# Splitting 32 weight blocks and the memory during the gates' stage, and a new order in the mixer's first group

## The chip, the cores and the metric

The kernel runs on one core of a Trainium2 chip. The time is device time in microseconds (us) of one execution, and a run's result is the median of its executions. A core has TensorE (PE, matmul; PEld is its weight load), VectorE (DVE), ScalarE (ACT), GpSimd (POOL) and SyncE (SP, which here only issues DMA loads). Each takes its instructions in order.

## The reference

Two blocks, 1024 tokens by 1024 features, all in fp32. The change touches the first block's gates and output, and the second block's mixer and cross-attention memory:

```python
m = sigmoid(g_att) * y_att + sigmoid(g_conv) * y_conv      # gates
x = x + m @ w_out                                          # first block's end, then a norm
proj = rmsnorm(x) @ w_in_2                                 # mixer: q_a k_a v_a q_i k_i w_i q_b k_b v_b
out_a = dsa_attention(...)   # index scores, top 256 keys of a query, softmax over those
out_b = diff_attention(...)  # (softmax(q1 k1) - lam softmax(q2 k2)) v, 4 heads
h = x + concat(out_a, out_b) @ w_out_2
k, v = rmsnorm(mem) @ w_xk, rmsnorm(mem) @ w_xv            # mem: 256 rows, for cross-attention
```

## The kernel before

A matmul of fp32 precision is made of three in fp32r: each operand is **split** into a high part (`hi`, an ACT copy that rounds, L130) and a low part (`lo = x - hi`, a DVE subtraction, L133, or L136 with a scale), and `mm3` (matmuls at L189) sums hi·hi, lo·hi and hi·lo. Activations and weights are both split, in tiles of 128 x 1024. `w` (L178) loads a weight block from DRAM into the one buffer `wr`, and splits it into `wh` and `wl` (two buffers each).

SBUF tiles come from tags with a fixed number of buffers: `U` 32, `P` 6, `PT` 4, `wr` 1, `wh` and `wl` 2, and in PSUM `S` 2, `T` 2, `A` 1, `D` 1. A new tile of a tag waits until an old one was read for the last time. `load` (L158) is a DMA issued by SP; it can be held back by `ago(ns)` until a matmul that lies that far back on PE. `dspill` (L174) stores a tile in DRAM by a DMA that POOL issues.

The stages in order of time, in us of the profiled execution:

- 358 to 675, **gates**: 16 iterations `end(n)` of seven products of four k-steps (a fast matrix product with sums of operands), 12 x 7 matmuls of 512 columns, 19.3 us each. PE's order is the written one. Sums and gate functions lie on DVE and ACT and use six `P` tiles; results go to DRAM.
- 675 to 807, the convolution's product, and **wo1**: `for d in range(8)` in `block1` multiplies by one block of w_out, adds x (`P`), splits the result into `hn2[d]` (`U`), sums its squares in `acc1` and `acc2` and spills it.
- 807 to 1086, **mixer projections**. A group (`tok_group`) has two weight blocks (`kh` 0 and 1, on hn2[0..3] and hn2[4..7]) and eight token tiles, 192 matmuls. The groups are w2b (196 columns: k_i, k_a, v_a, w_i), w2i (q_i), two each of w2q, w2k, w2v and w2a. `ahead` prepares weights two groups ahead, through `wr`, alternately into `U` and into `wh`, `wl`. In the w2b group `rms1` and `rms2` (column sums of acc1 and acc2 on PE, then DVE and POOL) give the factor `r12` with which all results are scaled. After w2i come the index scores (888 to 912), then 31 steps of the search for the top 256: one step counts on ACT (`jka`, three tiles) and DVE (`jkd`, three tiles) and updates the threshold `C`, on which the next step depends. The steps are woven between the groups' results, which `rope` copies from PSUM with ACT and turns on DVE. Before the last group `diff_prep` transposes q and k of the first head (L1126), for which a `T` buffer is needed.
- 1086 to 1500, **attention**: `diff`, 4 heads x 8 query tiles, with the last part of the search (`topk_final`), then `dsa`. Into it `weave` mixes at rate 0.43 `mem_in` (loads and splits the memory, sums its squares), `mem_kv` (16 weight blocks wkv, each loaded and split by `w`) and `ob_part`.
- then output products, cross-attention and the conv-GLU, which the change doesn't touch.

Except where the order is written (gates), a scheduler lays out each engine's and SP's order from the program's order and its own model of times.

Of the kernel before, what the change touches and what calls it, by code (L numbers as in the profile page):

```python
# [98 lines left out]
class Kernel:  # L99
# [216 lines left out]

    def mem_in(self, d, cost):

        m = []
        for q in range(2):  # L320
            x = self.big("U")
            self.load(x.rearrange("p (k c) -> p k c", k=4), self.I["memT"][4 * q:4 * q + 4].rearrange("k p c -> p k c"),
                      self.ago(4000))
            m += [x[:, c * 256:c * 256 + 256] for c in range(4)]
        for q in range(2):
            h, l = self.big("U", F32R), self.big("U", F32R)
# [84 lines left out]
    def tok_group(self, wv, x, ncols, small=False, inner=False, ws=None, mid=None):  # L411
# [390 lines left out]
    def mixer(self):  # L802
# [682 lines left out]
    def gates(self, attg):  # L1485
# [359 lines left out]
```

## Time and profile before

| | |
|---|---|
| median of 3 runs (lowest, highest) | 2467.7 us (2466.17, 2472.75) |
| the profiled execution's own time | 2467.37 us |
| its span | 2465.6 us |
| mean granted TensorE clock | 0.978 |
| busy: PE, DVE, ACT, POOL | 95%, 66%, 50%, 9% |

The span runs from the first to the last instruction; 1.8 us of the time lie around it. A granted clock of 1.00 is 2.4 GHz, 0.50 is 1.2 GHz. The shares are means over stages that differ much, so a stage is read from its own window.

### The profile page before, as it was taken

How to read it: one execution, taken by the hardware profiler on the slowest of the kernel's cores; microseconds unless marked ns; L12 is line 12 of the kernel's file. 1: busy time of each engine (PE TensorE's matmuls, PEld its weight loads, DVE VectorE, ACT ScalarE, POOL GpSimd, SP SyncE). 2: the span in 40 equal slices, each digit the busy share in tenths (PEclk: the TensorE clock that was granted, in tenths of full speed). 3: DMA queues.
4: the chain of work that ended last, by engine and by line, in shares of the span. 5: the costliest groups of instructions: out<-in, count | busy, mean ns of one | idle time of the engine just before them, and what ended most of it. 6: DMA issues, size and time to landing. Idle time of an engine off the chain costs nothing.

```text
span 2465.6 us, 32347 instructions
## 1 busy us (share of the span) xinstructions
PE 2340.9 (95%) x12324; PEld 1982.7 (80%) x12324; DVE 1631.2 (66%) x2666; ACT 1231.2 (50%) x2070; POOL 211.1 (9%) x318
## 2 busy tenths in 40 slices
PE   8999989999999899957798999999999999999999
PEld 7887878888888899956687777887878888888887
DVE  5476785565565478789976886435578888875433
ACT  4465554333433367788676764335454445543231
POOL 0000020000000114131111110000000000000000
PEclk9999999999999899989899999999999999999999
DMA  4323363312444222243452225212322222225554
GB/s 141 101 67 114 94 216 148 110 65 72 171 143 145 84 67 76 84 133 107 137 165 77 88 78 191 81 49 79 135 77 87 84 77 77 86 86 188 172 179 145
DMA packets 91548, 275.91 MB, mean 112 GB/s; under 512 B 11392, under 2 KB 16896, under 8 KB 91392
## 3 DMA queue, kind: packets, MB, share of 16 engines
q1 hardware_dynamic: 75168, 216.45, 27.2%
q0 software_dynamic: 15792, 57.15, 6.2%
q8 instruction: 97, 1.59, 0.3%
q14 instruction: 59, 0.48, 0.1%
q10 hardware_dynamic: 432, 0.23, 0.1%
HBM read 187.81 MB, written 64.49 MB: 102 GB/s over the span
## 4 chain that ended last, share of the span: by engine, by line
PE 74%; DVE 11%; ACT 6%; issue 4%; DMA 2%; POOL 2%; SPq 0%; DVEq 0%; ACTq 0%; POOLq 0%
PE S L189 39%; PE T L189 12%; PE D L189 11%; PE A L189 9%; DVE U L133 2%; PE T L493 2%; ACT jka L130 2%; DVE P L133 1%; ACT P L130 1%; DMA U<-sp 1%; DVE PT L133 1%; DVE jkd L1067 1%; DVE P L486 1%; ACT U L130 1%; POOL st L221 1%
## 5 line engine op out<-in xcount | busy, mean ns | idle before, releaser
L189 PE MATMUL S<-U,wh 128*128 128x512 f32 x1792 | 582.7, 392 | 18.5 <-ACT U L130 8.4
L189 PEld LDWEIGHTS S<-U,wh 128*128 128x128 f32 x1792 | 338.5, 189 | 92.7 <-ACT U L130 8.4
L189 PE MATMUL S<-U,wl 128*128 128x512 f32 x896 | 351.3, 392 | 2.9 <-DVE wl L133 2.9
L189 PE MATMUL D<-U,wh 128*128 128x512 f32 x816 | 281.3, 398 | 0.2
L130 ACT ACTIVATE wh<-wr 128x1024 fp32r<-128x1024 f32 (+1 forms) x113 | 112.7, 998 | 312.7 <-PE D L189 169.9
L133 DVE TENSOR_TENSOR wl<-wr,wh 128x1024 fp32r<-128x1024 f32 (+1 forms) x113 | 130.9, 1159 | 170.2 <-ACT wh L130 170.1
L189 PE MATMUL S<-U,U 128*128 128x256 f32 (+6 forms) x1040 | 216.0, 335 | 13.5 <-DVE st L486 12.7
L189 PE MATMUL S<-U,PT 128*128 128x512 f32 x912 | 224.8, 395 | 0.7 <-ACT jkd L130 0.7
L189 PEld LDWEIGHTS S<-U,PT 128*128 128x128 f32 x912 | 171.1, 188 | 41.9 <-ACT jkd L130 1.4
L189 PEld LDWEIGHTS S<-U,wl 128*128 128x128 f32 x896 | 169.4, 189 | 40.6 <-DVE wl L133 4.7
L189 PEld LDWEIGHTS S<-U,U 128*128 128x128 f32 x1040 | 159.5, 199 | 30.8 <-DVE st L486 14.5
L189 PEld LDWEIGHTS D<-U,wh 128*128 128x128 f32 x816 | 152.0, 188 | 29.6 <-DVE U L133 1.5
L189 PE MATMUL D<-U,wl 128*128 128x512 f32 x408 | 160.8, 394 | 0.4 <-DVE wl L133 0.4
L189 PE MATMUL T<-U,wh 128*128 128x512 f32 x480 | 161.0, 390 | 0.0
L189 PE MATMUL S<-wh,U 128*128 128x256 f32 x768 | 142.2, 287 | 0.0
L130 ACT ACTIVATE P<-P,st 128x640 f32<-128x640 f32 (+7 forms) x168 | 124.1, 739 | 35.8 <-DVE st L486 34.3
L130 ACT ACTIVATE PT<-T 128x512 fp32r<-128x512 f32 (+4 forms) x208 | 110.2, 544 | 53.7 <-PE T L493 46.5
L130 ACT ACTIVATE wh<-U 128x1024 fp32r<-128x1024 f32 x73 | 77.4, 1060 | 114.1 <-PE T L189 51.9
L133 DVE TENSOR_TENSOR wl<-U,wh 128x1024 fp32r<-128x1024 f32 x73 | 89.2, 1222 | 65.4 <-ACT wh L130 65.4
L133 DVE TENSOR_TENSOR PT<-U,PT 128x1024 fp32r<-128x1024 f32 x74 | 67.7, 955 | 97.7 <-PE S L189 97.7
L189 PE MATMUL A<-U,wh 128*128 128x512 f32 x368 | 125.1, 390 | 0.0
L189 PEld LDWEIGHTS S<-wh,U 128*128 128x128 f32 x768 | 122.2, 195 | 0.0
(298 smaller groups left out, 4660.7 us busy)
## 6 DMA issues: line engine op xcount, KB each, us to landing
U<-sp SPq DMA_DIRECT2D x73, 512.0 KB, 4.3
P<-sp SPq DMA_DIRECT2D x56, 512.0 KB, 4.5
sp<-P POOLq DMA_DIRECT2D x56, 512.0 KB, 2.9
sp<-U POOLq DMA_DIRECT2D x51, 512.0 KB, 3.5
U<-in_wf SPq DMA_DIRECT2D x43, 512.0 KB, 3.5
U<-in_w SPq DMA_DIRECT2D x30, 512.0 KB, 3.2
U<-U SPq DMA_DIRECT2D x116, 128.0 KB, 2.4
wr<-in_wf SPq DMA_DIRECT2D x23, 512.0 KB, 3.6
```

The costliest lines, as they stand in the source:

```text
L130: return self.nc.scalar.activation(out, in_, f, **kw)
L133: return self.nc.vector.tensor_tensor(out, a, b, op=op)
L189: self.last = self.nc.tensor.matmul(out, l, r, start=start, stop=stop, skip_group_check=True)
L221: self.nc.gpsimd.tensor_tensor(y, v, self.mhalf[:, :n], op=OP.pow)
L486: self.nc.vector.tensor_tensor_reduce(pv, v, add.rearrange("p (n x) -> p n x", n=n), scale, BIG, OP.add, OP.min, nm)
L493: self.nc.tensor.transpose(T[:, j * 128:j * 128 + 128], b, self.ident)
L1067: self.nc.vector.tensor_scalar(self.junk["d"][:, :w], SD[i], C[:, j:j + 1].bitcast(F32), None, op0=OP.is_lt, op1=OP.add, accum_out=cnt[:, ...
```

## The change

Of the weights, 16 blocks of the mixer (w2q, w2k, w2v, w2a) and the 16 blocks of wkv are now split early by `presplit`: loaded, split, and both parts stored in DRAM. 23 of them go into the gates' iterations (through `P`, one or two in an iteration, none in the last two), 9 into wo1 (through `U`). Later `parts` loads the two parts where the block was loaded and split before. The memory is split, squared and summed in gates n = 5 and 9 (`mem_split`). The low part is written over the loaded block. The weights of w2b are loaded and split in wo1 (d = 7). In the w2b group the second weight block's matmuls run k = 0..2 for all token tiles first, and k = 3, which reads hn2[7], last; rms1 comes after the first token tile of that pass, and rms2 after the fourth.

```diff
+    def presplit(self, key, tag):
+        ap = self.I[key[0]][key[1:]]
+        x, hi = self.load(self.big(tag), ap, self.ago(6000)), self.big(tag, F32R)
+        lo = x.bitcast(F32R)
+        self.split(hi, lo, x)
+        self.halves[key] = [self.dspill(v.bitcast(F32)) for v in (hi, lo)]
+
+    def parts(self, key, tags=("wh", "wl"), gate=None):
+        r = [self.t(t, [128, 1024], F32R) for t in tags]
+        for x, d in zip(r, self.halves[key]):
+            self.load(x.bitcast(F32), d, gate)
+        return r
...
+    def mem_split(self, q):
+        x, hi, sq = self.big("P"), self.big("P", F32R), self.big("P")
...
+        self.act(sq, x, AF.Square)
+        self.tt(sq[:, :512], sq[:, :512], sq[:, 512:], OP.add)
...
+        for c in range(4):
+            sl = slice(c * 256, c * 256 + 256)
+            self.split(hi[:, sl], lo[:, sl], x[:, sl], scale=self.gv("mem", 4 * q + c))
+        self.halves["mem", q] = [self.dspill(v.bitcast(F32)) for v in (hi, lo)]
...
-        for k in range(8):
-            self.split(*d[k], m[k], scale=self.gv("mem", k))
-            self.add_sq(acc, m[k], k == 0)
-            yield cost
+        acc = self.msq
+        yield cost
...
-                wh, wl = self.w(self.I["wkv"][which, h, kh])
+                wh, wl = self.parts(("wkv", which, h, kh))
...
+            if key + (kh,) in self.halves:
+                ws[kh] = self.parts(key + (kh,), (tag, tag) if tag else ("wh", "wl"))
+                continue
...
+        if mid is not None:
+            order[8:] = [(1, tt, range(3)) for tt in range(8)] + [(1, tt, range(3, 4)) for tt in range(8)]
...
+            if d == 7:
+                self.first = self.tok_weights(("w2b",), "U")
...
+            for _ in range((2, 2, 2, 2, 1, 0, 0, 0)[d]):
+                self.presplit(self.early.pop(0), "U")
...
+            for _ in range((1, 1, 2, 2, 2, 1, 2, 2, 2, 1, 2, 2, 2, 1, 0, 0)[n]):
+                self.presplit(early.pop(0), "P")
+            if n in (5, 9):
+                self.mem_split(n // 9)
```

**PE at the start of the w2b group.** `A` is the column sums, `S_6604` or `S_6932` the last product of wo1, `S_6716` or `S_7044` w2b's first PSUM tile. Before:

```order
L189 MATMUL S_6604<-U_6040,wh_6600 128x512
L189 MATMUL A_6815<-ones_108,P_6106 128x1 x8
L189 MATMUL S_6716<-U_6694,U_6168 128x196
L189 MATMUL S_6716<-U_6694,U_6169 128x196
L189 MATMUL S_6717<-U_6694,U_6168 128x196
```

The change, at the same place, and 104 matmuls of w2b later:

```order
L204 MATMUL S_6932<-U_6287,wh_6928 128x512
L204 MATMUL S_7044<-U_6983,U_6415 128x196
L204 MATMUL S_7044<-U_6983,U_6416 128x196
...
L204 MATMUL S_7044<-U_6990,U_6912 128x196
L204 MATMUL A_7152<-ones_108,P_6353 128x1 x8
L204 MATMUL S_7044<-U_6989,U_6763 128x196
```

The column sums moved behind 105 matmuls. At the group's end, 23 matmuls of w2i (`S_7409`) now stand between the transposes of k_i (`T_7291`) and of k_a (`T_7320`), which followed each other before.

**ACT in a gates iteration (n = 2, two presplit blocks).** `cs` and `jkd` are copies of the running sum in PSUM, which PE waits for; `wh`, `PT` are parts of the next iteration's left operand. Before:

```order
L130 ACTIVATE P_4013<-P_4013 128x1024
L130 ACTIVATE PT_4139<-U_4127 128x1024
L130 ACTIVATE wh_4123<-U_4121 128x1024
L130 ACTIVATE cs_110<-S_4068 128x512
L130 ACTIVATE wh_4133<-U_4129 128x1024
L130 ACTIVATE jkd_114<-S_4068 128x512
```

The change:

```order
L130 ACTIVATE P_4141<-P_4139 128x1024
L130 ACTIVATE P_4031<-P_4031 128x1024
L130 ACTIVATE wh_4159<-U_4157 128x1024
L130 ACTIVATE P_4150<-P_4148 128x1024
L130 ACTIVATE cs_110<-S_4086 128x512
L130 ACTIVATE PT_4175<-U_4163 128x1024
L130 ACTIVATE wh_4169<-U_4165 128x1024
L130 ACTIVATE jkd_114<-S_4086 128x512
```

The high parts of the two blocks (`P_4141`, `P_4150`) came in, the second right ahead of `cs`, and `PT` moved behind it.

**ACT at the last small group (w2a, first half), whose `T` buffers `diff_prep` needs.** `P<-T` are the copies that free them. Before, the copies and what is between them:

```order
L130 ACTIVATE P_9583<-A_9358,r_6851 128x256
L130 ACTIVATE jka_113,cnt_7548<-U_7349,C_7546 128x768
L130 ACTIVATE PT_9588<-P_9583 128x512
L130 ACTIVATE jka_113,cnt_7548<-U_7350,C_7546 128x896
L130 ACTIVATE P_9611<-T_9359,r_6851 128x256
```

The change:

```order
L130 ACTIVATE P_9851<-D_9653,r_7191 128x256 x2
L130 ACTIVATE PT_9856<-P_9851 128x512
L130 ACTIVATE P_9879<-A_9654,r_7191 128x256 x2
L130 ACTIVATE PT_9884<-P_9879 128x512
L130 ACTIVATE jka_113,cnt_7872<-U_7673,C_7870 128x768
L130 ACTIVATE P_9907<-T_9655,r_7191 128x256
```

The weight splits are gone from ACT and DVE between the groups, and fewer counts stand between the four tiles' copies.

## Rows read from the trace of the kernel before

**Rows 1.** The page's first part and its chain of waits: busy time, share of the span, instructions; the chain's shares by engine.

```profile
PE 2340.9 (95%) x12324; PEld 1982.7 (80%) x12324; DVE 1631.2 (66%) x2666; ACT 1231.2 (50%) x2070; POOL 211.1 (9%) x318
PE 74%; DVE 11%; ACT 6%; issue 4%; DMA 2%; POOL 2%; SPq 0%; DVEq 0%; ACTq 0%; POOLq 0%
```

**Rows 2.** Windows by stage: stretch, its length, busy us (instructions) of PE, PEld, DVE, ACT, POOL, granted clock, mean share of the DMA engines, GB/s.

```profile
375.00:655.00 280.00, 280.00 (x1221) 228.87 (x1220) 160.78 (x197) 103.45 (x133) 8.56 (x16) 1.00 0.29 105
719.00:763.00 44.00, 44.00 (x193) 35.94 (x192) 20.23 (x17) 14.74 (x14) 1.59 (x3) 1.00 0.35 120
...
807.00:846.00 39.00, 31.60 (x235) 31.03 (x235) 16.08 (x41) 12.94 (x26) 5.39 (x5) 0.87 0.20 66
846.00:888.00 42.00, 41.44 (x328) 40.76 (x327) 22.57 (x41) 13.73 (x31) 6.69 (x12) 0.96 0.54 150
...
912.00:1054.00 142.00, 142.00 (x1186) 142.00 (x1184) 114.94 (x281) 104.82 (x197) 46.84 (x64) 1.00 0.23 75
1054.00:1075.00 21.00, 0.24 (x4) 0.04 (x2) 16.54 (x46) 18.96 (x37) 5.27 (x10) 0.60 0.20 75
...
1100.00:1225.00 125.00, 94.37 (x617) 83.17 (x616) 117.23 (x279) 92.48 (x240) 27.71 (x28) 0.90 0.43 129
1225.00:1325.00 100.00, 84.92 (x573) 77.24 (x573) 66.38 (x155) 69.16 (x184) 13.41 (x20) 0.90 0.43 129
```

**Rows 3.** PE's waits from 800 to 1100: who waited for whom, us, times, the longest.

```profile
PE T L1126 <- ACT P L130: 20.8, 1, 20.8
PE A L189 <- DVE P L133: 5.0, 1, 5.0
```

**Rows 4.** PE's timeline at the w2b group: start, us, instruction, count, idle before it and what ended it.

```profile
812.08 3.40 PE L189 MATMUL A<-ones,P 128*128 128x1 f32 x16 [4.95 <-DVE P L133]
815.35 15.42 PE L189 MATMUL S<-U,U 128*128 128x196 f32 x120
830.60 1.86 PE L189 MATMUL A<-ones,P 128*128 128x1 f32 x16
...
842.44 0.62 PE L841 MATMUL T<-ident,P 128*64 128x128 f32 x4 [0.22 <-DVE P L133]
845.30 0.63 PE L841 MATMUL T<-ident,P 128*64 128x128 f32 x4 [2.23 <-DVE P L133]
```

**Rows 5.** Windows of 5 us, columns as in rows 2.

```profile
820.00:825.00 5.00, 5.00 (x47) 5.00 (x46) 0.90 (x1) 1.06 (x1) 0.00 (x0) 1.00 0.36 105
...
845.00:850.00 5.00, 4.70 (x27) 4.70 (x28) 3.99 (x12) 2.36 (x5) 2.01 (x5) 0.66 0.57 116
...
1075.00:1080.00 5.00, 5.00 (x29) 5.00 (x30) 4.72 (x15) 4.16 (x9) 2.08 (x5) 0.65 0.02 5
1080.00:1085.00 5.00, 5.00 (x44) 5.00 (x44) 4.76 (x15) 4.93 (x10) 2.40 (x5) 1.00 0.50 157
```

**Rows 6.** The timelines of DVE (first row: the last step to r12) and of ACT (second row: the first copy out of w2b's PSUM).

```profile
836.00 0.16 DVE L133 TENSOR_TENSOR r<-st 128x8 f32<-128x8 f32 x1
...
836.90 0.31 ACT L130 ACTIVATE U<-S,r 128x64 fp32r<-128x64 f32 x1 [6.93 <-PE S L189]
```

**Rows 7.** Groups by form from 888 to 1330: count, busy us, mean ns of one, idle before them.

```profile
L133 DVE TENSOR_TENSOR wl<-wr,wh 128x1024 fp32r<-128x1024 f32 x22 | 26.9, 1221 | 15.1 <-ACT wh L130 15.1
L130 ACT ACTIVATE wh<-wr 128x1024 fp32r<-128x1024 f32 x22 | 23.2, 1053 | 7.0 <-DMA wr<-in_w2v 3.0 <-DMA wr<-in_w2k 1.9 <-DMA wr<-in_wkv 1.8
...
L133 DVE TENSOR_TENSOR U<-wr,U 128x1024 fp32r<-128x1024 f32 x6 | 7.3, 1220 | 0.6 <-ACT U L130 0.6
...
L136 DVE SCALAR_TENSOR_TENSOR U<-U,gvec,U 128x256 fp32r<-128x256 f32 x8 | 3.8, 479 | 0.0
...
L133 DVE TENSOR_TENSOR PT<-PT,P 128x256 f32<-128x256 f32 x7 | 2.9, 415 | 0.0
```

**Rows 8.** The chain of waits from 871 to 875: start, us, what.

```profile
871.80 1.07 ACT wh L130
872.89 1.23 DVE wl L133
```

**Rows 9.** DVE's timeline, weight splits: the first and last of the 12 between 912 and 1075, then the first and last of the 7 between 1100 and 1225.

```profile
921.23 1.21 DVE L133 TENSOR_TENSOR U<-wr,U 128x1024 fp32r<-128x1024 f32 x1
...
1055.59 1.23 DVE L133 TENSOR_TENSOR wl<-wr,wh 128x1024 fp32r<-128x1024 f32 x1 [1.17 <-ACT wh L130]
...
1123.05 1.22 DVE L133 TENSOR_TENSOR wl<-wr,wh 128x1024 fp32r<-128x1024 f32 x1
...
1211.67 1.23 DVE L133 TENSOR_TENSOR wl<-wr,wh 128x1024 fp32r<-128x1024 f32 x1
```

**Rows 10.** A gates iteration: ACT's copy of the running sum (timeline), and PE's products around it (chain of waits).

```profile
412.58 0.60 ACT L130 ACTIVATE cs<-S 128x512 f32<-128x512 f32 x1 [0.98 <-PE S L189]
...
412.48 2.73 PE T L189 x12
415.21 8.32 PE S L189 x36
```

**Rows 11.** DMA issues from 375 to 655 (count, KB each, median us from issue to landing), and for wo1 (719 to 807) the rate in 40 equal slices of 2.2 us.

```profile
U<-in_w SPq DMA_DIRECT2D x28, 512.0 KB, 3.2
sp<-P POOLq DMA_DIRECT2D x16, 512.0 KB, 2.9
P<-sp SPq DMA_DIRECT2D x12, 512.0 KB, 5.1
...
GB/s 0 130 108 0 0 0 0 236 285 194 0 266 315 142 0 0 264 341 114 0 0 259 320 136 0 7 257 330 128 0 0 248 379 266 7 0 238 0 67 0
```

More of the change, by code (lines that the diff above doesn't have):

```diff
@@ L315, in rope_base @@
             self.act(self.cs[:, s], rr, AF.Sin)
+    def mem_split(self, q):
+        x, hi, sq = self.big("P"), self.big("P", F32R), self.big("P")
+        self.load(x.rearrange("p (k c) -> p k c", k=4), self.I["memT"][4 * q:4 * q + 4].rearrange("k p c -> p k c"),
+                  self.ago(6000))
+        self.act(sq, x, AF.Square)
+        self.tt(sq[:, :512], sq[:, :512], sq[:, 512:], OP.add)
+        if q == 0:
+            self.msq = self.const([128, 256], name="msq")
+            self.tt(self.msq, sq[:, :256], sq[:, 256:512], OP.add)
+        else:
+            self.tt(sq[:, :256], sq[:, :256], sq[:, 256:512], OP.add)
+            self.tt(self.msq, self.msq, sq[:, :256], OP.add)
+        lo = x.bitcast(F32R)
+        for c in range(4):
+            sl = slice(c * 256, c * 256 + 256)
+            self.split(hi[:, sl], lo[:, sl], x[:, sl], scale=self.gv("mem", 4 * q + c))
+        self.halves["mem", q] = [self.dspill(v.bitcast(F32)) for v in (hi, lo)]
     def mem_in(self, d, cost):
-        m = []
         for q in range(2):
[L321 to L326, printed above, removed]
-            d += [(h[:, c * 256:c * 256 + 256], l[:, c * 256:c * 256 + 256]) for c in range(4)]
-        acc = self.big("PT")[:, :256]
-        for k in range(8):
-            self.split(*d[k], m[k], scale=self.gv("mem", k))
-            self.add_sq(acc, m[k], k == 0)
-            yield cost
+            h, l = self.parts(("mem", q), ("U", "U"), self.ago(4000))
+            d += [(h[:, c * 256:c * 256 + 256], l[:, c * 256:c * 256 + 256]) for c in range(4)]
+        acc = self.msq
+        yield cost
         rm = self.mean_rsqrt(self.col_sums(acc, 2), 2, 1.0 / 1024)
@@ L422, in tok_group @@
             ws, self.pre = self.pre, {}
-        order = [(kh, tt) for kh in range(2) for tt in range(8)] if not inner else \
-            [(kh, 2 * q + z) for q in range(4) for kh in range(2) for z in range(2)]
-        for kh, tt in order:
+        order = [(kh, tt, range(4)) for kh in range(2) for tt in range(8)] if not inner else \
+            [(kh, 2 * q + z, range(4)) for q in range(4) for kh in range(2) for z in range(2)]
+        if mid is not None:
+            order[8:] = [(1, tt, range(3)) for tt in range(8)] + [(1, tt, range(3, 4)) for tt in range(8)]
+        for kh, tt, ks in order:
             if kh not in ws:
@@ L429, in tok_group @@
             sl = slice(tt * 128, tt * 128 + 128)
-            for k in range(4):
+            for k in ks:
                 xh, xl = x[kh * 4 + k]
@@ L435, in tok_group @@
                          f and tt % 2 == 0, kh == 1 and k == 3)
-            if mid is not None and (kh, tt) in mid:
-                mid[kh, tt]()
+            if mid is not None and (ks[-1], tt) in mid and kh:
+                mid[ks[-1], tt]()
         return views
@@ L820, in mixer @@
         VA = self.big("U", F32R)
-        groups = [lambda kh, n=n, g=g: I[n][g, kh] for n in ("w2q", "w2k", "w2v", "w2a") for g in range(2)]
-        todo = [lambda kh: I["w2b"][kh], lambda kh: I["w2i"][kh]] + groups
-        ready = []
+        todo = [("w2i",)] + [(n, g) for n in ("w2q", "w2k", "w2v", "w2a") for g in range(2)]
+        ready = [self.first]
         def ahead():
@@ L831, in mixer @@
         ws = ahead()
-        for t0, nt, ps in self.tok_group(None, hn2, 196, ws=ws, mid={(0, 7): self.rms1, (1, 1): self.rms2}):
+        for t0, nt, ps in self.tok_group(None, hn2, 196, ws=ws, mid={(2, 0): self.rms1, (2, 3): self.rms2}):
             self.v_split(ps[:, :, 128:192], t0, nt, VA.rearrange("p (t s d) -> p t s d", t=8, s=2)[:, t0:t0 + nt])
@@ L1490, in gates @@
         s3 = self.junk["d"].bitcast(F32)
-        w1, self.A, self.B = I["w1"], {}, [None] * 4
+        w1, self.A, self.B, self.halves = I["w1"], {}, [None] * 4, {}
+        early = [(n, g, kh) for n in ("w2q", "w2k", "w2v", "w2a") for g in range(2) for kh in range(2)]
+        early = self.early = early + [("wkv", z, x, kh) for x in range(4) for z in range(2) for kh in range(2)]
         Y, M, TH, CV = {}, {}, {}, {}
```

4 lines of the change are left out of this document (2 added, 2 removed).

## Prediction

> **What bounds the kernel now.** I read the page first, then windows by stage, then PE's waits, the timelines at those waits, and last the groups by form that price the edits. Over the whole span PE is 95% busy and 74% of the chain of waits [rows 1], so what isn't on PE is worth only what PE waits for it. The windows [rows 2] show where that is. In the gates (375 to 655) PE never stops, DVE works 161 of 280 us and ACT 103. From 807 to 846 PE is busy 31.6 of 39 us at a granted clock of 0.87. From 912 to 1054 PE is full again, but DVE (115 of 142) and ACT (105) fall behind it, and from 1054 to 1075 PE stands still while ACT works 19 of 21 us: the one wait of 20.8 us for the copies that free a `T` buffer [rows 3]. From 1100 to 1225 DVE is the full engine (117 of 125 us) and PE has 94; from 1225 to 1325 no engine is full (PE 85, ACT 69, DVE 66). So the split of a weight costs nothing in the gates and much between 860 and 1225, and that is what the change trades.
>
> **The w2b group (A).** Before, PE is free at 807.1 (812.08 less 4.95 idle), waits for DVE's sum of squares, does rms1, and only then w2b [rows 4]. Now 105 matmuls of w2b stand ahead of rms1, on hn2[0..6] and on weights split in wo1. At full clock 47 of them take 5 us [rows 5], 0.106 us each. So: 96 of kh = 0 end at 817.3, nine more at 818.3, rms1 (1.8 us by the second sum, rows 4) at 820.1, 27 more at 823.0, rms2 at 824.8, 36 at 828.6, and with 12 of the last pass the first PSUM tile is complete at 829.9, the second at 831.2. r12 came 3.7 us after the second sum's end (832.5 to 836.2) [rows 4, 6], so now at 828.5, before the tile. The first copy from PSUM followed r12 by 0.7 us [rows 6]; now it follows the tile, at 830.6 instead of 836.9: 6.3 us sooner. The transposes of k_i move with it, from 842.4 to 836.1, and w2i follows them at once, at 836.8, where it came after those of k_a, at 845.7: 8.9 us. Against that, PE now idles 4.9 us in one piece (831.2 to 836.1). After the waits of 0.2 and 2.2 us before 845 the granted clock was 0.66, with 27 matmuls in 5 us where 44 fit at full clock [rows 4, 5], 1.9 us lost. I charge 1 us more for the longer idle time. A is -8 us, at worst -5 (the copies slower than before by 3 us), at best -11. The Trainium skill (TensorE: Matmul & The Clock Gate, section "What's actually happening") says the array's default is the lower clock and only activity releases it; by that rule alone the new idle time would cost a ramp of its own, 1.9 us, and A would be -7. The trace agrees that a wait ends at 0.66 and 0.65.
>
> **The projections (B).** Two kinds of splits leave. One w2q split lies on the chain just before the index scores, 1.07 us on ACT and 1.23 on DVE [rows 8]: -2.3. Then 12 splits leave DVE and ACT between 921 and 1056 [rows 9], each 1.22 us busy on DVE and 1.05 on ACT [rows 7]; ACT also stands 4.9 us for the loads of w2v and w2k (3.0 and 1.9). DVE's relief is 12 x 1.22 = 14.6 us, ACT's 12 x 1.05 + 4.9 = 17.5. Both engines take part in the chain; I take the smaller, less 0.6 for overlapping ends: 14. PE's work doesn't change, so PE's lead over ACT at the transposes, 20.8 us, shrinks by 2.3 + 14 to 4.5. After the long wait the clock was 0.65 with 29 matmuls in 5 us, then 44 [rows 5]: 15 matmuls of 0.114 us, 1.7 us, come back. B is -18. Best: the whole wait goes, -22.5. Worst: only the last four splits count, because up to there the results come from PE at PE's pace, which is full [rows 2]: 4 x 1.22, -5.
> The weights now come as two loads of 512 KB instead of one and go straight into `wh` and `wl` or `U`. Such a load waits on SP until PE has read the old part, and all loads behind it on SP wait too (q's moved halves are among them). It costs nothing as long as a group's lead holds: 192 matmuls of 0.114 us, 22 us, against 5.1 us for a load [rows 11].
>
> **The attention (C).** From 1100 to 1225 DVE loses 7 weight splits (8.5 us), the memory's 8 scaled splits (3.8) and 7 sums (2.9) [rows 7, 9]: 15.2 us. It idles only 7.8 us there. What stands beneath it is PE with 94 us of 125 at 0.90 [rows 2], so most can come out: I take two thirds, -10. From 1225 to 1325 seven or eight more splits leave, but no engine is full and the waits there are those of head changes: -2. C is -12; at best both in full, -24, at worst -3, if the moved halves and loads at the head changes set the pace.
>
> **What is put into the gates and wo1 (D).** DVE gets 23 x 1.22 = 28 us and ACT 23 x 1.06 = 24, plus some 4 us each for each half of the memory, against 119 and 177 us of idle time [rows 2]: no engine becomes full. What counts is in-order delay. ACT's high part of a block stands ahead of `cs`, the copy that PE needs before it adds the next product. `cs` ends at 413.2 and PE comes back to that tile at 415.2 [rows 10]: 2.0 us of cover, against 1.06 for the copy, if its load has landed. In a two-block iteration the second load goes out when DVE has read an old `P` tile, and has some 5 us to land, against 3.2 us for a weight and 5.1 for a stored tile [rows 11]. So a few iterations may pay 1 us, and the two with the memory 1 each. POOL gets 46 stores there at no computing of its own to delay. In wo1, eight blocks in 44 us add 8 x 1.57 MB (one load, two stores) to 120 GB/s: 406 GB/s, over the best slice of 379 [rows 2, 11]. That leaves 1.2 MB late, 3 us at that rate, and it drains in the second half of wo1, where the added traffic is one block. A late weight is hidden, since `wr` is loaded about one d (11 us) ahead. D is +4, between 0 and the rival below.
>
> **Sum.** -8 - 18 - 12 + 4 = -34. Against the profiled execution, 2467.4 us, which lies 0.3 under the median: 2433 us. Its own range, from the terms' bounds taken half way: 2418 to 2449.
>
> **Rivals.**
> *The search, not the splits (smaller gain).* The chain of 31 threshold steps and PE's pace hold DVE and ACT, and the splits filled gaps. For it: PE is full from 912 to 1054, and DVE idles 27 us there [rows 2]. Against it: ACT is 90% busy when PE waits. Then B is -5 and C half, -6: 2467 - 8 - 5 - 6 + 4 = 2452 us.
> *Everything comes out (larger gain).* The wait goes whole, the attention falls to PE's work at a better clock: -9 - 22.5 - 24 + 1, 2413 us. For it speaks that PE has 31 us idle from 1100 to 1225.
> *The gates give way (slower).* The extra tiles share six `P` buffers, each freed only when its store has landed, and ACT waits in order for a presplit load that comes late; then `cs` is late and PE stops, in each of 14 iterations. It decides once PE loses 2.7 us per iteration (38 us in all, the -34 with D's 4 put back), that is, once the load lands 3.6 us late (2.7, and the 0.9 that the copy leaves of the cover). If in two-block iterations the store, the load and the copy follow one another (2.9 + 5.1 + 1.1 = 9.1 us in a gap of 5), 4 us are lost each time: 14 x 4 = 56, and the time is 2467 - 38 + 56 = 2485 us. Against it: the idle share of DVE and ACT, and a store's 2.9 us at 57% busy DVE. The Trainium skill (SBUF — State Buffer, section "SBUF: two separate sides") has a rule on this side: a DMA issued from POOL can stall because VectorE holds the shared port and its descriptors can't be written. By it each store could start a DVE instruction late, an estimate of 1.2 us, which the cover takes; the 16 stores of this stage, at 2.9 us, don't show it.
>
> **How the numbers follow.** The forecast has 0.60, the smaller gain 0.20, the larger 0.10, the slower 0.10. About 0.3%, 7.4 us, can be told from no change, so faster means below 2460. The forecast and the larger gain give nearly all their share to faster, the smaller gain 0.16 (the rest, with B and C at their worst, is same), the slower rival 0.09 to slower: faster 0.86, same 0.05, slower 0.09. The range from 2412 to 2458 leaves out about half of the larger gain, a quarter of the smaller and the slower rival: 0.2.
>
> **What would show it.** A: no wait of 5 us before the column sums, w2i's start near 837. B: the wait for `T` under 8 us and no clock below 0.9 after it. C: the stretch from the row sums of the first softmax to the end of the second head shorter by about 10 us, with DVE under 90%. D: gates iterations still 19.3 us, with PE without waits for `cs` and wo1 still 88 us. Wrong would be: waits of PE for ACT in the gates, or a wait for `T` that stays above 15 us.

## The result and the profile after

The changed kernel took 2450.6 us (median of 4, 2446.0 to 2454.1), the kernel before 2469.4: a ratio of 0.9923, 95% interval 0.9900 to 0.9945, 18.8 us less. In a second set of runs (E5 below) it took 2446.2 against 2472.3, a ratio of 0.9894 (0.9874 to 0.9914). The forecast was 2433, some 35 us less, with a range from 2412 to 2458: the sign and the range are right, the gain is half to three quarters of what was forecast.

The page of the changed kernel has the same work on the engines as before [rows 1], but for POOL's stores:

```profile
PE 2342.5 (96%) x12324; PEld 1983.2 (81%) x12324; DVE 1632.7 (67%) x2664; ACT 1233.4 (50%) x2064; POOL 236.4 (10%) x386
```

The part of the program ahead of the first mark below differs by up to 7 us from run to run, and most of that lies ahead of the gates. So I compare stages, from PE's timelines, with five marks: the one product of the convolution that waits 0.75 us for ACT (at 669.57 before, 669.68 after; in E6 and E8 it waits 1.20 and 1.64 us, so their sums leave out up to 0.9 us), the end of wo1, w2i's first matmul, the transposes of the row factors that begin the attention, the first of wo2's matmuls behind it, and the end of the span. Lengths in us, of the profiled execution of each run (E1 and so on are the experiments below):

| | wo1 | w2b group | w2i, search, projections | attention | rest | sum | wait for T | ratio to before |
|---|---|---|---|---|---|---|---|---|
| before | 137.6 | 38.5 | 255.1 | 382.4 | 982.4 | 1796.0 | 20.8 | |
| forecast, from the terms | 141.6 | 30.5 | 237.1 | 370.4 | 982.4 | 1762.0 | 4.5 | 0.986 |
| changed | 139.4 | 36.0 | 249.1 | 370.9 | 984.1 | 1779.5 | 10.7 | 0.9923 |
| E5 changed again | 137.6 | 35.5 | 249.0 | 371.0 | 980.5 | 1773.5 | 10.8 | 0.9894 |
| E1 w2b alone | 137.6 | 33.3 | 257.5 | 380.6 | 982.9 | 1791.8 | 21.5 | 0.9968 |
| E2 + w2 blocks | 137.6 | 30.0 | 248.3 | 381.4 | 983.6 | 1780.9 | 11.0 | 0.9929 |
| E3 no splits in wo1 | 137.6 | 30.0 | 248.2 | 382.3 | 982.4 | 1780.5 | 10.8 | 0.9926 |
| E4 sums spread | 137.6 | 32.3 | 249.2 | 370.4 | 977.8 | 1767.3 | 10.8 | 0.9888 |
| E6 splits even | 137.6 | 32.1 | 251.0 | 371.8 | 981.1 | 1773.6 | 10.8 | 0.9905 |
| E7 fewer rounds before | 138.7 | 35.0 | 236.1 | 400.5 | 977.5 | 1787.9 | 0 | 0.9965 |
| E8 spread and even | 137.6 | 30.6 | 249.3 | 370.3 | 982.2 | 1770.1 | 10.7 | 0.9886 |
| E9 counts moved | 138.7 | 36.8 | 244.9 | 367.9 | 981.0 | 1769.4 | 7.3 | 0.9898 |
| E10 last nine early | 137.6 | 33.3 | 248.7 | 382.4 | 986.0 | 1787.9 | 10.8 | 0.9947 |
| E11 E8 and E9 | 137.6 | 30.7 | 243.7 | 369.8 | 977.8 | 1759.5 | 7.6 | 0.9859 |
| E12 E3, k and v in U | 137.6 | 33.3 | 250.5 | 385.1 | 985.0 | 1791.5 | 10.7 | 0.9926 |

The rest, which no kernel changes, goes from 977.5 to 986.0; a sum is good to some 4 us. A stage that two runs have with the same instructions repeats to less than one, but for wo1 (changed, E5) and the w2b group (E1, E2). So the attention gave what was forecast, the w2b group and the projections did not. The kernel before was run beside each set of runs; between sets the ratios are compared.

**Gates and wo1.** The windows that answer to [rows 2]:

```profile
375.00:655.00 280.00, 280.00 (x1221) 228.78 (x1219) 193.37 (x234) 130.46 (x168) 35.07 (x66) 1.00 0.69 246
...
763.00:809.00 46.00, 44.74 (x194) 35.79 (x192) 29.04 (x26) 21.24 (x21) 7.43 (x14) 1.00 0.89 337
809.00:846.00 37.00, 30.52 (x233) 29.90 (x233) 17.39 (x46) 11.94 (x24) 3.65 (x3) 0.87 0.35 121
```

In the gates PE is busy 280.00 of 280 us with 33 us more work on DVE and 27 more on ACT: the splits there are free. ACT did stand 9.6 us there for late loads of wkv blocks (three times), and PE did not notice. In wo1's first half (719 to 763) 219 GB/s move, in its second half 337 at 89% busy DMA engines, and that shows behind it.

**The w2b group.** PE's timeline, columns as in [rows 4]:

```profile
808.96 0.41 PE L204 MATMUL S<-U,U 128*128 128x196 f32 x2
810.64 5.38 PE L204 MATMUL S<-U,U 128*128 128x196 f32 x46 [1.27 <-DVE U L133]
816.92 6.61 PE L204 MATMUL S<-U,U 128*128 128x196 f32 x57 [0.90 <-DVE P L133]
823.37 1.86 PE L204 MATMUL A<-ones,P 128*128 128x1 f32 x16
825.09 4.82 PE L204 MATMUL S<-U,U 128*128 128x196 f32 x27
829.70 1.96 PE L204 MATMUL A<-ones,P 128*128 128x1 f32 x16
831.52 8.55 PE L204 MATMUL S<-U,U 128*128 128x196 f32 x60
...
844.38 1.06 PE L874 MATMUL T<-ident,P 128*64 128x128 f32 x4 [4.31 <-DVE P L133]
845.10 0.78 PE L204 MATMUL S<-wh,U 128*128 128x256 f32 x2
```

The order is the forecast's: w2b ahead of the column sums, w2i right behind the transposes of k_i. But w2i starts at 845.1, not 837. wo1 ends 1.9 us later: PE waits there twice for the low part of a w_out block, 0.69 and 0.57 us. Two new waits, 2.2 us together, stand at the start of w2b, one for the low part of w2b's first weights and one for a PSUM tile that wo1's last add had not yet read. And 27 matmuls behind the first sums take 4.6 us (825.09 to 829.70), 0.17 each, where the 46 ahead of them take 0.117. And w2i starts at half clock, behind the 4.31 us in which PE waits; the window to set beside 0.66 in [rows 5]:

```profile
845.00:850.00 5.00, 5.00 (x26) 4.97 (x23) 2.77 (x10) 1.22 (x3) 2.75 (x5) 0.50 0.26 56
```

DVE's timeline shows the waits' origin:

```profile
803.70 1.22 DVE L133 TENSOR_TENSOR P<-P,S 128x1024 f32<-128x1024 f32 x1 [2.07 <-DMA P<-in_xT]
...
814.75 0.98 DVE L133 TENSOR_TENSOR U<-wr,U 128x784 fp32r<-128x784 f32 x1 [2.02 <-ACT U L130]
815.65 1.22 DVE L133 TENSOR_TENSOR P<-P,S 128x1024 f32<-128x1024 f32 x1
```

wo1's last add (815.65; 807.17 in the kernel before, just behind PE's product) stands in order behind the split of w2b's second weights, which stands behind ACT's split of them and so behind their load (ACT waits 5.01 us for it), and the add before it waits for x. x took 9.2 us from issue to landing in wo1 (first line), 5.5 where no block is split in wo1 (second line, E3):

```profile
P<-in_xT SPq DMA_DIRECT2D x7, 512.0 KB, 9.2
```

```profile
P<-in_xT SPq DMA_DIRECT2D x7, 512.0 KB, 5.5
```

**The wait for T.** PE still waits 10.73 us (a row of its timeline), and its clock is low again behind the wait (a window, columns as in [rows 2]):

```profile
1064.81 1.11 PE L1159 MATMUL T<-ident,U 128*128 128x128 f32 x4 [10.73 <-ACT P L130]
...
1065.00:1070.00 5.00, 5.00 (x29) 5.00 (x29) 4.96 (x16) 4.24 (x10) 2.78 (x5) 0.62 0.00 0
```

ACT's timeline shows what frees the `T` buffers after PE's last product at 1054.08:

```profile
1055.40 1.04 ACT L130 ACTIVATE jka<-U,C 128x896 int8<-128x896 f32 x1
1056.35 0.19 ACT L130 ACTIVATION_READ_ACCUMULATOR jka<-U,C 128x1 f32 x1
1056.57 1.15 ACT L130 ACTIVATE jka<-U,C 128x1024 int8<-128x1024 f32 x1
1057.62 0.19 ACT L130 ACTIVATION_READ_ACCUMULATOR jka<-U,C 128x1 f32 x1
1057.71 0.82 ACT L130 ACTIVATE P<-D,r 128x256 f32<-128x256 f32 x2
...
1064.30 0.46 ACT L130 ACTIVATE P<-T,r 128x256 f32<-128x256 f32 x1
```

No split is left, and the copies still stand behind rounds of counts (`jka`). A round is a chain: counts, a comparison, the new threshold `C`, the next counts. POOL's `Cn` marks each; the changed kernel:

```profile
1028.91 0.20 POOL L1110 TENSOR_TENSOR Cn<-C,step 128x6 int32<-128x6 int32 x1 [3.84 <-DVE C L136]
1032.94 0.20 POOL L1110 TENSOR_TENSOR Cn<-C,step 128x6 int32<-128x6 int32 x1 [3.84 <-DVE C L136]
1036.98 0.20 POOL L1110 TENSOR_TENSOR Cn<-C,step 128x6 int32<-128x6 int32 x1 [3.83 <-DVE C L136]
```

The kernel before had rounds as short where no split fell into them:

```profile
1057.25 0.19 POOL L1077 TENSOR_TENSOR Cn<-C,step 128x6 int32<-128x6 int32 x1 [2.82 <-DVE C L136]
1061.27 0.20 POOL L1077 TENSOR_TENSOR Cn<-C,step 128x6 int32<-128x6 int32 x1 [3.83 <-DVE C L136]
1065.30 0.20 POOL L1077 TENSOR_TENSOR Cn<-C,step 128x6 int32<-128x6 int32 x1 [3.83 <-DVE C L136]
```

4.03 us is the period of a round that nothing else lengthens, and it could be read before. (In the changed kernel 7 of the 24 distances ahead of the wait are 4.02 to 4.04 us; a few shorter ones, down to 3.08, stand beside longer ones.) From the first `Cn` to the 25th went 147.6 us before and 136.2 after; the difference of 11.4 us is about what the wait lost (20.8 to 10.7).

**A load that moved back.** From the end of that wait to the row factors went 25.8 us before and 29.4 after. SP's timeline of the changed kernel: the second of the first head's loads (`U<-sp`, here k) now stands behind the moves of q's halves (L496 to L498), at 1078.38; before, SP issued it at 1057.27, ahead of them. (SP issues these moves too, not loads alone.) PE waits for it:

```profile
1075.84 2.49 SPq L498 DMA_DIRECT2D U<-PT  x2
1078.38 0.74 SPq L158 DMA_DIRECT2D U<-sp  x1
```

```profile
1083.43 1.06 PE L1159 MATMUL T<-ident,U 128*128 128x128 f32 x8 [2.57 <-DMA U<-sp]
```

**The attention.** The window from the row factors on, 125 us long as in [rows 2]:

```profile
1093.00:1218.00 125.00, 99.34 (x655) 88.67 (x654) 109.69 (x269) 82.83 (x225) 25.14 (x31) 0.89 0.61 192
```

DVE went from 117 to 110 us there, PE's matmuls from 617 to 655. How far each kernel has come shows in DVE's row sums of the softmaxes: the last of `diff`'s second head, the last of its fourth, and the eighth of `dsa`. Before (row factors at 1100.79):

```profile
1196.12 1.28 DVE L486 CUSTOM_DVE_ANT_0 P<-S,U,rqb 128x1024 f32<-128x1024 f32 x1
1292.86 1.28 DVE L486 CUSTOM_DVE_ANT_0 P<-S,U,rqb 128x1024 f32<-128x1024 f32 x1
1313.98 0.35 DVE L486 CUSTOM_DVE_ANT_0 U<-S,U,rqa 128x128 f32<-128x128 f32 x1
```

The change (row factors at 1094.16):

```profile
1185.32 1.28 DVE L516 CUSTOM_DVE_ANT_0 P<-S,U,rqb 128x1024 f32<-128x1024 f32 x1
1263.37 1.28 DVE L516 CUSTOM_DVE_ANT_0 P<-S,U,rqb 128x1024 f32<-128x1024 f32 x1
1298.09 0.35 DVE L516 CUSTOM_DVE_ANT_0 U<-S,U,rqa 128x128 f32<-128x128 f32 x1 [0.90 <-PE S L204]
```

Counted from the row factors the change is 4.2 us ahead at the end of the second head, 22.9 ahead at the end of the fourth, and 9.3 ahead at `dsa`'s eighth sum. What it gives back there is PE's work: between `dsa`'s first sum and its eighth stand 142 matmuls, PE busy 20.7 of 25.8 us, where before there were 51 in 10.9 us.

### The profile page after: what moved, and what is told of

Read it like the earlier page. It is cut to its first block, busy times and chain, and to the rows that moved or that the text cites. A ratio compares the mean times of both kernels' runs of the same rounds, so it can differ in the third digit from the quotient of the medians.

```text
span 2449.2 us, 32676 instructions
## 1 busy us (share of the span) xinstructions
PE 2342.5 (96%) x12324; PEld 1983.2 (81%) x12324; DVE 1632.7 (67%) x2664; ACT 1233.4 (50%) x2064; POOL 236.4 (10%) x386
## 4 chain that ended last, share of the span: by engine, by line
PE 45%; DVE 5%; ACT 4%; DMA 3%; issue 3%; POOL 1%; SPq 0%; DVEq 0%; ACTq 0%; POOLq 0%
PE S L204 22%; PE T L204 8%; PE A L204 6%; PE D L204 6%; ACT jka L130 2%; DMA U<-sp 2%; PE T L523 1%; DVE U L133 1%; DVE P L133 1%; ACT P L130 1%; POOL st L236 1%; ACT PT L130 1%; ACT U L130 1%; DMA U<-U 1%; DVE PT L133 1%
## 5 line engine op out<-in xcount | busy, mean ns | idle before, releaser
L130 ACT ACTIVATE wh<-wr 128x1024 fp32r<-128x1024 f32 (+1 forms) x89 | 87.4, 982 | 266.3 <-PE D L204 171.1
L133 DVE TENSOR_TENSOR wl<-wr,wh 128x1024 fp32r<-128x1024 f32 (+1 forms) x89 | 101.6, 1142 | 149.2 <-ACT wh L130 148.7
L204 PEld LDWEIGHTS S<-U,U 128*128 128x128 f32 x1040 | 160.5, 200 | 32.3 <-DVE st L516 12.5
L204 PEld LDWEIGHTS D<-U,wh 128*128 128x128 f32 x816 | 153.0, 189 | 29.4 <-DVE U L133 0.8
L174 POOL DMA_DIRECT2D sp<-P x106 | 56.8, 536 | 816.5 <-DVE P L133 549.2
L133 DVE TENSOR_TENSOR P<-P,P 128x1024 f32<-128x1024 f32 (+3 forms) x105 | 119.6, 1148 | 18.9 <-ACT P L130 18.7
L133 DVE TENSOR_TENSOR U<-U,U 128x512 f32<-128x512 f32 (+3 forms) x146 | 114.7, 800 | 23.5 <-ACT U L130 22.8
L130 ACT ACTIVATE P<-P 128x1024 f32<-128x1024 f32 (+2 forms) x105 | 101.5, 968 | 48.5 <-DVE P L133 23.6
```

Source lines behind the costliest of these rows:

```text
L130: return self.nc.scalar.activation(out, in_, f, **kw)
L133: return self.nc.vector.tensor_tensor(out, a, b, op=op)
L174: self.nc.gpsimd.dma_start(dt, src)
L204: self.last = self.nc.tensor.matmul(out, l, r, start=start, stop=stop, skip_group_check=True)
```

## The experiments

**E1, the w2b part alone.** All counts of early blocks are zero, no `mem_split`, and `mem_in`, `mem_kv` take their old code.

```diff
-            for _ in range((1, 1, 2, 2, 2, 1, 2, 2, 2, 1, 2, 2, 2, 1, 0, 0)[n]):
+            for _ in range((0, 0, 0, 0, 0, 0, 0, 0, 0, 0, 0, 0, 0, 0, 0, 0)[n]):
```

> Only the w2b part of the change: no block and no memory is split early (those are loaded and split where they were before), the weights of w2b come early, the order in the w2b group is the new one. Theory 'crowded wo1' (the nine blocks split in wo1 make the loads of x and of w2b's second weights late, and with them the last add of wo1; the clock after the column sums takes the rest): wo1 ends at 807 again, PE has no wait of 1.27 and 0.90 us at the start of w2b, the first column sums run at 818 to 819 instead of 823.4, and w2i starts at 840 to 841 (845.1 in the changed kernel, 845.7 before). The time is some 5 us under the kernel before, 2464. The forecast's own term (no loss at all): w2i at 837 and 8 us, 2461. Rival 'the order itself' (the copies behind the last pass set the start of w2i, whatever DMA does): w2i at 844 to 845, time within 1.5 us of the kernel before.

Measured: 2462.1 against 2471.1 (0.9968, 0.9951 to 0.9985). wo1 is as before, no wait stands at the start of w2b, the column sums run 2.7 us sooner after wo1 than in the changed kernel, and w2i starts 5.3 us sooner than before, which is the theory's 840 to 841. What is missing to the 8.5 us of E2 and E3 is the clock: behind the first sums it fell to 0.59. The time, 9.0 us under the kernel before, is nearer to the forecast's 2461 than to the theory's 2464 and can't tell them apart. The next stage is 2.4 us longer than before, though no split has left it: 1.6 us of that lie between w2i and the first `Cn`.

**E2, the w2 blocks as well.** 16 blocks in the gates.

```diff
+            for _ in range((1, 1, 2, 2, 2, 1, 2, 2, 2, 1, 0, 0, 0, 0, 0, 0)[n]):
```

> As e1_w2b_alone, and the 16 blocks of w2q, w2k, w2v and w2a are split in the gates; wkv and the memory as before. It is compared with e1. Theory 'the search' (ACT takes the copies that free the T buffers only behind the counts of the search, and at 4.03 us a step the search is a chain of its own, which no split lengthens): PE still waits 10 to 11 us for T, the last twelve steps before that wait are 4.03 us apart, and e2 is 6 to 8 us under e1. The forecast: the wait is under 5 us and e2 is 18 us under e1. Rival 'the splits filled gaps': e2 within 3 us of e1.

Measured: 2455.3 (0.9929, 0.9908 to 0.9951), 6.8 under E1; the wait for T is 11.0 us. That is the theory of the search, not the forecast. Its w2b group took 30.0 us: the same instructions as in E1, but the clock held. So 3.3 us of the difference to E1 are the clock's; the stage from w2i on is 9.2 us shorter than in E1.

**E3, no splits in wo1.**

```diff
-            for _ in range((2, 2, 2, 2, 1, 0, 0, 0)[d]):
+            for _ in range((0, 0, 0, 0, 0, 0, 0, 0)[d]):
...
+                wh, wl = self.parts(key) if key in self.halves else self.w(self.I["wkv"][which, h, kh])
```

> The changed kernel without the nine blocks split in wo1: the last nine blocks of wkv are loaded and split where they were before. Theory 'crowded wo1': wo1 ends at 807, no waits at the start of w2b, w2i starts at 840 to 841, 4 to 5 us sooner than in the changed kernel; the nine splits that return lie behind 1200, where DVE is not full, and cost 2 to 4 us; so the time is 0 to 3 us under the changed kernel. Rival 'wo1 is innocent': w2i at 844 to 845 again, and the nine splits cost 2 to 7 us: 2 to 7 us over the changed kernel.

Measured: 2453.9 (0.9926, 0.9901 to 0.9950). wo1's part came as expected: no waits, a w2b group of 30.0 us. The attention was missed: the nine returned splits cost 11.4 us, all that the attention had won (382.3), where 2 to 4 were expected. By the ratios the time is that of the changed kernel in its first set.

**E4, the column sums spread.** One one-column matmul behind every three matmuls of w2b, from the second token tile of the second pass on.

```diff
+    def spread(self, z):
+        ps = self.t("AD"[z], [128, 512])
+        for j in range(8):
+            self.mm(ps[:, j:j + 1], self.acc12[z][:, j * 128:j * 128 + 128], self.ones[:, 0:1], j == 0, j == 7)
+            yield
+        (self.rms1, self.rms2)[z](ps[:, :8])
...
+                if mid is not None and kh and (k > 2 or tt):
+                    next(mid, None)
```

> The changed kernel with the 16 column sums spread over the second weight block's pass, one behind every three matmuls of w2b, the second sum in its own PSUM tag. Theory 'the clock falls behind a run of column sums': the granted clock stays at 0.95 or more from 823 to 840, where the changed kernel has two stretches of 3 us at 0.52 to 0.55; PE comes to the end of w2b some 3 us sooner; r12 comes later (its last sum is 33 matmuls before the end), so w2i starts at 842 to 843.5 (845.1 in the changed kernel), and the time is 2 us lower. Rival 'the clock falls there for another reason': the two stretches stay, w2i at 845 or later.

Measured: 2444.3 (0.9888, 0.9870 to 0.9907). Windows of 3 us (columns as in [rows 2]) of the changed kernel, then of E4:

```profile
824.00:827.00 3.00, 3.00 (x26) 3.00 (x27) 0.00 (x0) 0.23 (x1) 0.00 (x0) 0.91 0.50 180
827.00:830.00 3.00, 3.00 (x17) 3.00 (x16) 1.50 (x3) 0.82 (x1) 0.00 (x0) 0.52 0.00 0
...
833.00:836.00 3.00, 3.00 (x18) 3.00 (x17) 0.24 (x2) 0.00 (x0) 2.07 (x1) 0.55 0.98 340
```

```profile
824.00:827.00 3.00, 3.00 (x28) 3.00 (x28) 0.03 (x1) 0.03 (x1) 0.00 (x0) 1.00 0.61 180
827.00:830.00 3.00, 3.00 (x30) 3.00 (x28) 1.50 (x3) 1.03 (x1) 0.00 (x0) 1.00 0.00 0
...
833.00:836.00 3.00, 3.00 (x29) 3.00 (x29) 0.10 (x2) 0.00 (x0) 2.87 (x1) 1.00 0.99 370
```

The stage is 3.2 to 3.7 us shorter than in the two executions of the changed kernel, and w2i starts 169.9 us behind the first mark, where 172.3 to 173.8 was expected. By the ratios the time is some 9 us under the first set of the changed kernel and 1.5 under E5, so the stage shows the gain and the time alone would not. wo1 had the same nine splits and took 137.6 us: the loss there comes in some executions only (the changed kernel, E7 and E9 lost 1.1 to 1.9 us, E4 and E5 nothing), and in none of the eight runs with fewer splits in wo1.

**E5, the changed kernel again.**

> The changed kernel itself, once more, beside the next three on the same chip. If what it lost at the w2b group (1.9 us in wo1, then waits of 1.27 and 0.90 us, then 3.0 us to the clock behind the column sums) is fixed by its instructions, w2i starts 175.4 us after the end of the convolution's input wait (the landmark at 669.7) again. If the clock's part is a matter of the execution, as the runs without early splits suggest (there one kernel lost 3.8 us and two 0.5 with the same instructions), the waits of about 2 us return and the clock's loss lies anywhere from 0 to 4 us: w2i at 171 to 176.

Measured: 2446.2 (0.9894). The waits returned, wo1's 1.9 us did not, and the clock took as much again: w2i 173.0 us behind the first mark.

**E6, splits spread evenly.**

```diff
+            for _ in range((1, 1, 1, 1, 1, 1, 1, 0)[d]):
...
+            for _ in range((2, 1, 2, 2, 2, 1, 2, 2, 2, 1, 2, 2, 2, 1, 1, 0)[n]):
```

> The changed kernel with its 32 blocks spread otherwise: 25 in the gates' iterations (two in the first, one in n = 14), one in each of d = 0 to 6 of wo1, instead of 23 and 9 (two in each of d = 0 to 3). Theory 'crowded wo1': with 1.57 MB more in 11 us instead of 3.1 MB the loads of x land in 6 us instead of 9, wo1 is 137.6 us behind the landmark again, the two waits at the start of w2b (2.2 us) go or fall under 1 us, and the time is 2 to 4 us under the changed kernel of the same call. Rival 'it is the number of splits in wo1, not their place': the waits stay at about 2 us, the time is the same within 1.5 us.

Measured: 2446.1 (0.9905, 0.9887 to 0.9924), the same as E5 within 1.5 us. The waits at w2b's start went (1.7 us in E5) and the stage is 3.4 us shorter, the other half of it because the clock fell once behind the sums and not twice; but the projections took 2.0 us more: a local gain, not one in the time.

**E7, fewer rounds ahead of the copies.**

```diff
-                some(2)
+                some(1)
             par += 1
```

> The changed kernel with one step of the search instead of two behind each result of the w2v groups: 20 instead of 26 rounds of counts stand ahead of the copies that free the T buffers; the six go behind them. Theory 'the search' (the copies wait in ACT's order behind counts, 4.03 us a round): six rounds are 24 us, more than PE's lead, so PE's wait for T falls from 10.7 us to under 2, and the last projections end 7 us sooner; in the first heads of the attention, where DVE is full, the six rounds (2.7 us of DVE each) take back 3 to 10 us of it. Time 0 to 4 us under the changed kernel. Rival 'the copies wait for something else' (a load of weights, a P tile): the wait for T stays above 8 us.

Measured: 2463.1 (0.9965), 17 us over E5. The wait for T is gone and the projections are 12.9 us shorter: the copies did wait for the rounds. But the attention is 29.5 us longer, for six rounds, and I had allowed 10. The largest of PE's waits there:

```profile
PE T L1159 <- DMA U<-sp: 15.8, 4, 7.9
PE A L204 <- ACT PT L130: 9.1, 12, 1.7
```

It is for the heads' loads of q and k (3.4 us in E5 from 1055 on), not for DVE. That is 12.4 of the 29.5 us; where the rest lies, and how a round brings the wait about, was not tried.

**E8, E4 and E6 together.**

> e4_spread_sums and e6_even_splits together: the column sums spread over the second pass, and at most one block split in a d of wo1. If both theories hold, no wait and no loss to the clock is left ahead of the transposes of k_i but the one of 4 to 5 us for the copies: w2i starts 169 us behind the landmark (175.4 in the changed kernel, 169.9 in e4), and the time is 4 to 8 us under the changed kernel of this call. If the spread sums won by chance in their first run, the gain is that of e6_even_splits alone.

Measured: 2443.0 (0.9886, 0.9871 to 0.9901), 3.2 under E5 and just short of the 4 to 8. The w2b group takes 30.6 us, with under 0.5 lost to the clock; w2i starts 168.2 us behind the first mark.

**E9, the counts dealt out otherwise.**

```diff
-    ACT_TILES = (5, 6, 7)
+    ACT_TILES = (2, 6, 7)
...
+        self.SH = {5: self.SC[5], 4: half(x[3], 512)[:, 384:1024], 3: half(x[5], 768)}
```

> The changed kernel with the counts of the search dealt out otherwise: ACT counts the tiles of 384, 896 and 1024 columns, DVE those of 512, 640 and 768 (before: ACT 768, 896, 1024; DVE 384, 512, 640). Theory 'the search' (behind 1000 us the rounds of ACT's counts are a chain of their own at 4.03 us, and the copies that free T stand in it): ACT's part of a round is some 0.3 us shorter, DVE's 0.4 us longer and still under ACT's, so a round takes 3.7 us; over the last 12 to 25 rounds ahead of the copies that is 4 to 7 us, the wait for T falls from 10.7 to 4 to 7 us, and the time is 4 to 6 us under the changed kernel. Rival 'DVE is as late as ACT': a round stays at 4.0 us and nothing moves.

Measured: 2444.8 (0.9898, 0.9869 to 0.9928). The rounds and the wait moved as expected:

```profile
1027.55 0.20 POOL L1110 TENSOR_TENSOR Cn<-C,step 128x6 int32<-128x6 int32 x1 [3.52 <-DVE C L136]
1031.27 0.20 POOL L1110 TENSOR_TENSOR Cn<-C,step 128x6 int32<-128x6 int32 x1 [3.52 <-DVE C L136]
1034.99 0.20 POOL L1110 TENSOR_TENSOR Cn<-C,step 128x6 int32<-128x6 int32 x1 [3.52 <-DVE C L136]
```

```profile
PE T L1159 <- ACT P L130: 7.6, 2, 7.3
```

A round is 3.72 us, PE's wait 7.3, projections and attention 7.2 us shorter than in E5 (4.1 and 3.1; in E11 the attention does not repeat it). The whole time does not show it: this execution lost 2.4 us in wo1 and the w2b group, which it does not change.

**E10, the last nine blocks of wkv alone.** The memory and the first seven as before.

```diff
+        early = self.early = early + [("wkv", z, x, kh) for x in range(4) for z in range(2) for kh in range(2)][7:]
```

> The other half of e3_no_wo1_splits: the memory and the first seven blocks of wkv are as before, and the last nine are split early (25 blocks in the gates, none in wo1). The forecast's weights (10 us from the full DVE of the first stretch, 2 from the second): the attention from the transposes of the row factors to the output product takes 380 us, 2 under the kernel before (382.4), since the stretch with the full DVE is unchanged. Theory 'the second stretch' (the nine splits lie between the head changes and cost what e3 gave back): 370 to 375 us. The time: 2 us or 8 to 12 us under e2_w2_in_gates, which was 15.8 us under the kernel before.

Measured: 2457.0 (0.9947, 0.9933 to 0.9961). The attention took 382.4 us: nothing, near the forecast's weight of 2. E3 and E10 are the two halves of one edit; neither gains anything alone, and both together gain 11.5.

**E11, E8 and E9 together: the version to keep.**

> e8_spread_and_even and e9_counts_moved together. If the gains add, w2i starts at 168 to 170 us behind the landmark, the wait for T is 4 to 7 us, and the time is 4 to 6 us under e8, some 33 us under the kernel before. If the search only hands PE's lead back elsewhere (the attention starts sooner, and the last rounds of the search then fall into its first head), it is within 2 us of e8.

Measured: 2434.0 us (2431.0 to 2442.9; 0.9859, 0.9827 to 0.9892), 36 us under the kernel before. By the ratios that is 7 us under E8, by the medians 9; only four runs were made, and the highest is as long as E8's median. The gains add: w2b group 30.7, wait for T 7.6, projections 5.6 us shorter than in E8. The stages up to wo2 are some 6 us shorter, the upper end of the expected 4 to 6; another 4.4 lie in the rest, which the edit doesn't touch.

**E12, k and v of the memory in U.** E3's chain of waits passes a store from a `P` buffer:

```profile
1257.90 9.49 DMA sp<-P
1267.53 1.15 DVE P L517
```

```diff
-            res = self.t("P", [128, 1024], F32R)
+            res = self.t("U", [128, 1024], F32R)
```

> e3_no_wo1_splits with one tag changed: the results k and v of the memory, which are stored to DRAM, take U buffers instead of P. In e3 the attention from the transposes of the row factors to the output product was as long as in the kernel before (382.3 and 382.4 us; 370.9 in the changed kernel) although the memory and seven of its sixteen weight splits had gone; its chain of waits there passes a store from a P buffer of 9.5 us, for which DVE stands 4.8 us. Theory 'the stores hold the P buffers': that wait goes, and the stretch takes 371 to 377 us, the time is 5 to 11 us under e3. Rival 'the nine splits themselves are late': 380 to 384 us, the time within 3 us of e3.

Measured: 2449.6 (0.9926, 0.9907 to 0.9945), the ratio of E3, as the rival had it; the attention took 385.1 us, outside both ranges. DVE's wait went, and the attention up to dsa's first product took 210.7 us for 217.4; but from there to wo2 it took 174.5 for 164.9. The profiled execution was the slowest of its five (2465.0), so it settles nothing: why neither half of the edit gains alone stays open.

## Why the forecast was half right

**A, the w2b group: -8 forecast, -2.5 and -3.0 measured.** The mechanism is right at its full size: where DMA and the clock take nothing (E2, E3), w2i starts 8.5 us sooner. Two steps failed. "At full clock ... 0.106 us each": behind the column sums it isn't full; PE's busy time times one less the granted clock, summed over the stage in windows of 4 us, is 3.5 us in the changed kernel, under 0.5 in E2, E3 and with the sums spread. (The 0.106 was also read too low: the window counts matmuls that lie across its edges. Where the clock holds, in E3, they start 0.112 us apart, 1.1 us more over 192.) I had charged nothing for the sums, though the kernel before shows it too: its 120 matmuls between the two sums took 15.2 us, 0.127 each [rows 4]. Those stand behind a wait of 4.95 us as well; behind its second sums there is no wait, and the clock fell:

```profile
833.00:836.00 3.00, 3.00 (x16) 3.00 (x16) 0.08 (x2) 0.00 (x0) 2.88 (x1) 0.50 0.33 134
```

The 1 us more that I charged for the idle time is about right, but it is paid behind w2i's start, in the next stage: 0.50 where it was 0.66. And "a late weight is hidden": late it was, with x, and the last add of wo1 stands behind it on DVE: 2.2 us of waits, gone in E1, E3 and E6. Of the idle time before the transposes the forecast said 4.9 us; it was 4.3. And E1's next stage, 2.4 us longer, says that the new order hands on some of its gain.

**B, the projections: -18 forecast, -6.0 and -6.1 measured.** The step that failed is "PE's lead over ACT, 20.8 us, shrinks by 2.3 + 14 to 4.5". I took the splits for the load and the rounds for what fits around them. The rounds are the chain: 12 splits gave 11.4 us of it by the 25th round, and the period of 4.03 us a round keeps 10.7 us of the wait (E2: the same; E9: a shorter round, a shorter wait; E7: fewer rounds ahead, no wait). The -2.3 of the split on the chain ahead of the index scores did not appear: from w2i to the first `Cn` it took 1.0 us more, of which the half clock at w2i's start is 0.9. The 1.7 us of clock behind the wait did not come back either: 0.65 before, 0.62 now. And 3.5 us were given back behind the wait, 2.6 of them to the load that SP now issues later. I had named that queue and priced it at nothing. Set against E1, which has the new order alone, the splits of this stage are worth 9.2 us (E2), half of the 18.

**C, the attention: -12 forecast, -11.5 and -11.4 measured.** The sum is right, and that is luck: its division, -10 for the stretch with the full DVE and -2 for the next, is wrong. The sign named for it, the second head's end 10 us sooner, came as 4; the third and fourth heads gave 18.7 us, with which the change was 22.9 ahead, near the bound of 24 that I had for both in full, and PE's work at the start of `dsa` took 13.6 of that back (E5 repeats it). Nor do the halves add: at the end of `diff` E3 is 7.7 us ahead of the kernel before and E10 1.6, and at `dsa`'s eighth sum E3 is 2.2 behind and E10 1.4 ahead. At the end of `diff` E12 is 9.9 us ahead of E3: that points to the wait for the stores as a part, and leaves open what is lost behind it.

**D: +4 forecast, +1.9 and 0.0 in wo1, nothing in the gates.** The slower rival fell: PE did not wait once in the gates' window. Most of the price of wo1's splits stood in the next stage. I had reckoned with 406 GB/s over the first half of wo1; the windows show 219 there and 337 in the second half, where x and w2b's weights are loaded. The Trainium skill (Perfetto Trace Analysis, section "Roofline") puts the ceiling of a core's 16 DMA engines at some 435 GB/s; slices of 1.5 us between 740 and 800 reached 426, so it agrees.

The time lies on the rival "the search, not the splits" (2452), for half its reason: B as that rival had it (-6 for -5), but C as the forecast (-11.5 for -6) and A far from both (-2.5 for -8). That the sum agrees is chance. And the forecast's own range is added up wrongly: its terms' bounds taken half way, with D between 0 and 4, give 2422 to 2446, not 2418 to 2449.

## What to carry to other kernels

Before work is taken off an engine, find the period of the loop that is left on it: a chain of dependent rounds has one of its own, which can be read in the trace of the kernel before (here 4.03 us between two `Cn`), and here what was taken out beside it gave back no more than the difference to it. Move work to a stage by its own idle time, and look at the first in-order instructions of the stage after it, too: wo1's splits were paid in the w2b group. Where two edits relieve one stretch, try each alone and both. And check the parts of a term that came out right: C was right only as a whole.

## What the runs showed of the hardware

The granted clock fell to half while PE was busy by its records, behind a run of 16 matmuls of one column: in the changed kernel to 0.52 (827 to 830), with PE 3.00 of 3.00 us busy. Of ten profiled executions of the changed kernel and its variants with the sums in a run, eight lost 2.0 to 3.8 us of the w2b stage to the clock and two (E2, E3) under 0.5, E2 with the same instructions in this stage as E1; the three with the sums spread (E4, E8, E11) lost under 0.5. If two in ten escape by chance, three of three do so about once in a hundred times. The Trainium skill (TensorE: Matmul & The Clock Gate, section "What's actually happening") says that how many matmuls run at the lower clock differs from run to run of one kernel; E1 and E2, alike in this stage, agree.
